# Output tiles of a gated delta-rule layer: beside all chunks of the recurrence, or beside the last two and behind it

## The chip, the cores and the metric

The kernel runs on one core of a Trainium2 chip. The core has five engines that work at the same time, each through its own list of instructions and strictly in the order of that list: TensorE (PE in the profile, matmuls and transposes; PEld is its loading of weights), VectorE (DVE), ScalarE (ACT), GpSimd (POOL) and SyncE (SP), which here only issues DMA transfers. Engines wait for each other by semaphores. The metric is the device time of one execution in microseconds (us); the time of a kernel is the median of its runs.

## The reference

The program is one inference step of a two-layer hybrid encoder for 2048 prompt tokens and 32 sample tokens of width 1024. The change lies in the first layer, a gated delta rule with 8 heads of width 128. Cut to what matters:

```python
def delta_layer(x, conv_buf, s0, w_in, conv_w, a_log, dt_bias, norm_w, w_out, ln_g, ln_b):
    proj = x @ w_in
    qkv, new_buf = causal_conv(proj[..., :CONV_DIM], conv_buf, conv_w)
    z = proj[..., CONV_DIM:CONV_DIM + A_VW].reshape(b, l, A_HEADS, A_DV)
    ...
    o, s_new = gated_delta_rule(q, k, v, g, beta, s0.astype(jnp.float32))
    o = o * lax.rsqrt(jnp.mean(o * o, -1, keepdims=True) + RMS_EPS) * norm_w * jax.nn.silu(z)
    out = o.reshape(b, l, A_VW).astype(x.dtype) @ w_out
    return layer_norm(DN_ALPHA * x + out, ln_g, ln_b), new_buf, s_new.astype(x.dtype)

# gated_delta_rule, one block of positions after another, for each head
    lower = jnp.where(strict, jnp.einsum('nbhik,nbhjk->nbhij', kbeta, kc) * decay, 0.0)
    # u, w: solutions of (lower + 1) against v * beta and k * beta * exp(gcum)
    def step(s, xs):
        v_new = ui - jnp.einsum('bhck,bhkv->bhcv', wi, s)
        o = jnp.einsum('bhck,bhkv->bhcv', qd, s) + jnp.einsum('bhij,bhjv->bhiv', ai, v_new)
        s = s * gl[..., None, None] + jnp.einsum('bhck,bhcv->bhkv', kd, v_new)
        return s, o
```

The second layer (windowed attention with a gate) takes the first layer's output `h` and begins with projections of it.

## The kernel before

The program goes through stages. `P1` makes the projections of the first layer. `z`, the gate product, is a projection of its own (`P1.z`, L211 to L225): for each of 8 heads and each block of 416 tokens 24 matmuls of 128x416, then tanh on ACT and two operations on DVE. Blocks 0, 1 and 2 of `z` are done before the delta stage, blocks 3 and 4 are put beside it.

The delta stage (`Delta.run`) goes through 17 chunks: 16 of 128 prompt tokens and one of 32 sample tokens. What a chunk needs is made two chunks ahead, in these steps:

- `lower` (L400 to L405): the products `g` of the keys on PE, in two halves; DVE multiplies them by the decays `E` into `npr`; after the second half ACT copies the diagonal 32x32 blocks to `nb`.
- `chain` (L414 to L423): DVE transposes `nb` to `L`; then 62 small steps on POOL, two for each of 31 rows (`tm`, L421, and `Tt`, L423), invert all those blocks.
- `spread` (L479 to L492): when the chain has ended, DVE transposes `Tt` to `tcp` and `ucp`, and ACT copies them into the matrices `t` and `u` in four pieces each.
- `invert` (lines L509 to L534, tile `bps`): small matmuls on PE, with copies between them, put the 32x32 inverses together to 128x128.
- `turn_k`, `turn_v` and `inside` (L433 to L467): transposes of `k` and `v`, and the products `gq` of `q` and `k`.
- `errors` and `advance` (L544 to L581): the step itself, on the state `Sp`: `ks`, `vp`, `vs`, then `op` and `sp`, with `o` copied by ACT and its squares summed there.
- `scale` and `emit`: the normalized `o` is transposed, multiplied by `z` and stored as `s_g` (L611).

Buffers come from pools. `L`, `tm`, `nb` and others lie in a pool with one buffer, `Tt` in one with two. One buffer means that the next write to the tile waits until the last reader of the one before is done.

The output tiles (class `O1`) compute `layer_norm(ALPHA * x + out)` for 128 tokens each: 17 tiles. `fetch` (L726 to L730) loads `s_g` of a tile into `g` and the rows of `x` into `r`. `split` (L737, L738) splits `g` into `g_hi` (a cast on ACT) and `g_lo` (a subtraction, on POOL). `tile` has two halves of 512 columns; each is 8 k-steps of three matmuls 128x512 (L751 to L753: `g_hi` by `wo_hi`, `g_hi` by `wo_lo`, `g_lo` by `wo_hi`), and then DVE does the residual, the statistics and the normalization. Finally `turned` (L790 to L803) transposes the tile in eight pieces (L797, tile `tr`), ACT and DVE copy four of them each to `hT`, and `hT` is stored, since the next stage reads the tokens in its columns. `hT` and `g` share one buffer (tag `g` of the one-buffer pool). The transposes have a PSUM bank of their own, the products `po` two. The constructor loads the output weights in eight pieces (L699 to L701).

The next stage is `P2`, the second layer's projections; it loads `hT` by blocks of 416 tokens as `act_raw` (L860) and weights by `slab`. Two of its gate products (`gate(0, (0,))` and `gate(0, (1,))`) need only the first blocks of `hT` and are run among the last output tiles.

The order of the work is set in two ways. On DVE, ACT, POOL and SP a scheduler orders the instructions by a simulation of the program. On PE, in `with tc.manual_schedule(engines={PE})`, the order is that in which the code issues: the delta rule's steps, and between them a `Filler`. `Filler.give(us)` adds `us` to what is owed and draws the generator `beside()` until its steps, each of which names its own length, have paid for it. `beside()` is first the gate products of blocks 3 and 4, then the output tiles; an output tile waits until the chunk of the tile after it has been issued (`sent`). In `run` each step is followed by a call of `fill` with a share of `more`, 0.8 up to the last two chunks and 1.6 there. Behind the last chunk `filler.rest()` draws what is left.

Of the kernel before, what the change touches and what calls it, by code (L numbers as in the profile page):

```python
# [10 lines left out]
F32 = mybir.dt.float32  # L11
# [3 lines left out]
ALU = mybir.AluOpType  # L15
AX = mybir.AxisListType
PSUM = bass.MemoryType.PSUM
# [312 lines left out]
class Delta:  # L330
# [282 lines left out]

    def run(self, chunks, fill, done):

        n = len(chunks)
        at = lambda i: chunks[i] if i < n else None

# [31 lines left out]
        for i, ch in enumerate(chunks):  # L650
            nx, n2 = at(i + 1), at(i + 2)
            more = 0.8 if n2 else 1.6
            if n2:
# [24 lines left out]
            g = self.inside(n2, V) if n2 else iter(())  # L678
# [34 lines left out]
class OutNorm:  # L713
# [18 lines left out]
    def split(self, got, n):  # L732
        nc = self.nc
        g, r = got
        ghi = self.two.tile([128, KC, 128], F32R, tag="g_hi", name="g_hi")
        glo = self.two.tile([128, KC, 128], F32R, tag="g_lo", name="g_lo")
        nc.scalar.copy(ghi[:, :, :n], g[:, :, :n])  # L737
        nc.gpsimd.tensor_tensor(out=glo[:, :, :n], in0=g[:, :, :n], in1=ghi[:, :, :n], op=ALU.subtract)  # L738
        return ghi, glo, r
# [40 lines left out]
class O1:  # L780
    def __init__(self, tc, es, I, O, T, G):
        self.nc, self.I, self.T, self.G = tc.nc, I, T, G
        self.on = OutNorm(tc, es, "o1", "left", I, "a", 2)
        self.pt = new_pool(tc, es, "o1_pt", 1, PSUM, side="left")

# [3 lines left out]
    def turned(self, h, c0, row, n):  # L789
# [3 lines left out]
        for q in range(2):  # L793
            tr = self.pt.tile([128, 4, 128], F32, tag="tr", name="tr")
            for j in range(4):
                k = q * 4 + j
                nc.tensor.transpose(tr[:, j, :n], h[:n, k * 128:k * 128 + 128], self.G["ident"][:n, :n])  # L797
            if q == 0:
                nc.scalar.copy(hT[:, 0:4, :n], tr[:, :, :n])
            else:  # L800
                nc.vector.tensor_copy(hT[:, 4:8, :n], tr[:, :, :n])
                nc.sync.dma_start(T["hT"][:, :, c0:c0 + n].rearrange("h p t -> p h t"), hT[:, :, :n])
            yield 0.44  # L803

    def tiles(self, tiles, ready, more):
# [3 lines left out]
        got = self.on.split(self.fetch(*tiles[0]), tiles[0][2])  # L809
        for i, t in enumerate(tiles):  # L810
            while not all(ready(u) for u in tiles[i + 1:i + 2]):
                yield 1.0
# [11 lines left out]
            if i + 2 == len(tiles):  # L824
                yield from more(0)
        yield from more(1)
        yield from late


class P2:  # L830
# [3 lines left out]
    def __init__(self, tc, right, I, O, T):  # L834
# [8 lines left out]
        self.x = {}  # L843
        self.w = {}
        for b in (0, 1):
            self.load(b, self.resr)
# [336 lines left out]
def program(tc, I, O, T, G):  # L1183
# [10 lines left out]

    def beside():
        yield from p1.z((3, 4), zp, ("zth", "z"), p1.left_ps, nc.vector)
        left.close()
        o1.append(O1(tc, left, I, O, T, G))
        tiles = [(t * 128, t * 128, min(128, NT - t * 128)) for t in range(NTT)]
        yield 20.0  # L1200
        yield from o1[0].tiles(tiles, lambda t: t[0] in sent, first_gate)

    def first_gate(b):
        yield from p2.gate(0, (b,), p2.ps)

    filler = Filler(beside())
    chunks = [Chunk(t * 128, 128) for t in range(16)] + [Chunk(NP, NS)]

    def done(ch):
        sent.add(ch.t0)  # L1210

    with tc.manual_schedule(engines={mybir.EngineType.PE}):
        delta.run(chunks, filler.give, done)
        right.close()
        p2 = P2(tc, right, I, O, T)
        p2.slab(0, nc.gpsimd)
        p2.slab(1, nc.gpsimd)
        filler.rest()
    left.close()
    p2.open_left(left)  # L1220
    drain(p2.gate(1, (0, 1), p2.ps))
# [174 lines left out]
```

## Time and profile before

| what | value |
|---|---|
| time, runs | 2402.85, 2398.37, 2401.82 us; median 2401.82 |
| profiled execution | 2404.43 us, of which the span of its instructions 2402.4 |
| PE | 2228.8 us busy, 93% of the span |
| PEld | 2029.5 us, 84% |
| DVE | 1392.3 us, 58% |
| POOL | 929.5 us, 39% |
| ACT | 898.5 us, 37% |

The busy shares are means over stages with different limits. The page's table of 40 slices shows PE at nine tenths or more in most slices and at seven to eight in the slices from about 840 us on, where the delta stage runs; POOL is busy for five to seven tenths there. The stage lies between about 712 us (the first chunk's preparation) and 1521.6 us (the last matmul of an output tile).

Rows of the trace read as start, length, engine, line, operation, out<-in with the tiles' names, shape; in square brackets stands the idle time before the instruction and what ended it. Groups read as count, busy time, mean length in ns, and idle time before them with what ended it.

### The profile page before, as it was taken

To read this page: it belongs to the slowest core of one execution; us is meant where nothing else is said; L and a number is where in the kernel's file an instruction comes from. 1 tells how busy PE (TensorE), PEld (TensorE's weight loads), DVE (VectorE), ACT (ScalarE), POOL (GpSimd) and SP (SyncE) were. 2 spreads that over 40 slices of the span, in tenths; PEclk is the share of its full clock that TensorE was granted. 3 is DMA by queue.
4 is the path that set the end of the run, shared out by engine and by line. 5 is a ranking of instruction groups with operands and counts; after the bars stand their busy time and mean duration, and the time that the engine had idled before them with its cause. 6 is when DMAs were issued, how large, how long until landed. Compare 5 with 4: busy or idle time off the path is not lost. (4 is left out here: it accounts for less than half of the span.)

```text
span 2402.4 us, 36689 instructions
## 1 busy us (share of the span) xinstructions
PE 2228.8 (93%) x13778; PEld 2029.5 (84%) x13778; DVE 1392.3 (58%) x2648; ACT 898.5 (37%) x2197; POOL 929.5 (39%) x1413
## 2 busy tenths in 40 slices
PE   7999999999989968888878897999999998999997
PEld 5999999999988857777777785899999986788885
DVE  3676666544437667777766766413444225667874
ACT  3344444333224454545444432221111235444451
POOL 1422212111203356565766644103433134555663
PEclk9999999999999979999898998999999999999998
DMA  5111211121236374555454446422222266233221
GB/s 181 62 73 67 76 71 63 71 80 67 100 105 139 94 189 83 134 119 118 120 129 102 123 125 191 146 80 101 68 74 75 75 154 178 80 97 106 88 67 57
DMA packets 268593, 247.79 MB, mean 103 GB/s; under 512 B 67600, under 2 KB 243792, under 8 KB 265072
## 3 DMA queue, kind: packets, MB, share of 16 engines
q1 hardware_dynamic: 259168, 233.50, 34.1%
q10 hardware_dynamic: 9248, 11.96, 1.6%
q8 instruction: 108, 1.77, 0.3%
q14 instruction: 69, 0.57, 0.1%
HBM read 154.57 MB, written 91.20 MB: 102 GB/s over the span
## 5 line engine op out<-in xcount | busy, mean ns | idle before, releaser
L69 PE MATMUL ps<-act_hi,w_hi 128*128 128x416 f32 x2000 | 708.6, 355 | 2.7 <-ACT w_hi L50 2.0
L71 PE MATMUL ps<-act_hi,w_lo 128*128 128x416 f32 x2000 | 702.6, 352 | 0.0
L70 PE MATMUL ps<-act_lo,w_hi 128*128 128x416 f32 x2000 | 701.9, 351 | 0.2 <-DVE act_lo L61 0.2
L69 PEld LDWEIGHTS ps<-act_hi,w_hi 128*128 128x128 f32 x2000 | 376.2, 188 | 8.6 <-ACT w_hi L50 2.3
L70 PEld LDWEIGHTS ps<-act_lo,w_hi 128*128 128x128 f32 x2000 | 377.0, 189 | 4.6 <-DVE act_lo L61 0.6
L71 PEld LDWEIGHTS ps<-act_hi,w_lo 128*128 128x128 f32 x2000 | 376.1, 188 | 5.5
L51 POOL TENSOR_TENSOR w_lo<-w_raw,w_hi 128x1024 fp32r<-128x1024 f32 x54 | 143.7, 2661 | 609.5 <-ACT w_hi L50 557.9
L421 POOL TENSOR_TENSOR tm<-L,Tt 128x60 f32<-128x60 f32 (+26 forms) x496 | 184.9, 373 | 261.4 <-DVE L L414 194.6
L180 DVE SCALAR_TENSOR_TENSOR y<-R,convw,y 128x2083 f32<-128x2083 f32 x72 | 171.6, 2384 | 121.1 <-ACT y L178 119.8
L423 POOL TENSOR_TENSOR Tt<-Tt,tm 128x60 f32<-128x60 f32 (+26 forms) x496 | 195.0, 393 | 38.5
L1140 POOL TENSOR_TENSOR P<-P,sm 128x384 f32<-128x384 f32 (+2 forms) x128 | 103.5, 830 | 159.3 <-DVE sm L1017 85.1
L210 ACT COPY R<-ps 128x416 f32<-128x416 f32 (+1 forms) x144 | 61.4, 449 | 208.4 <-PE ps L71 184.2
L1013 ACT ACTIVATE P<-S,nm 128x192 f32<-128x192 f32 (+2 forms) x260 | 104.7, 420 | 90.9 <-DVE nm L1006 43.7
L50 ACT CAST w_hi<-w_raw 128x1024 fp32r<-128x1024 f32 x62 | 65.0, 1049 | 193.5 <-PE ps L70 154.8
L880 POOL TENSOR_TENSOR rs<-rs,sin 128x416 f32<-128x416 f32 x50 | 71.3, 1426 | 147.4 <-DVE rs L879 103.0
L751 PE MATMUL po<-wo_hi,g_hi 128*128 128x512 f32 (+1 forms) x272 | 120.1, 441 | 0.0
L753 PE MATMUL po<-wo_hi,g_lo 128*128 128x512 f32 (+1 forms) x272 | 109.5, 402 | 0.0
L752 PE MATMUL po<-wo_lo,g_hi 128*128 128x512 f32 (+1 forms) x272 | 109.3, 402 | 0.0
L1153 PE MATMUL ot<-pt,vd 128*128 128x256 f32 x372 | 98.8, 392 | 3.5 <-DVE graw L1156 1.6
L1038 PE MATMUL po<-wo_hi,g_hi 128*128 128x512 f32 x240 | 100.0, 417 | 1.3 <-ACT wo_hi L700 1.3
L1039 PE MATMUL po<-wo_lo,g_hi 128*128 128x512 f32 x240 | 96.9, 404 | 2.1 <-DVE wo_lo L701 2.1
L566 PE MATMUL op<-Sp,q 128*128 128x128 f32 (+1 forms) x272 | 61.6, 313 | 37.4 <-ACT o L570 30.8
(263 smaller groups left out, 4187.1 us busy)
## 6 DMA issues: line engine op xcount, KB each, us to landing
w_raw<-in_w_in SPq DMA_DIRECT2D x40, 512.0 KB
w_raw<-in_b_w_in SPq DMA_DIRECT2D x20, 512.0 KB
s_z<-z SPq DMA_DIRECT2D x40, 208.0 KB
s_bz<-za SPq DMA_DIRECT2D x40, 208.0 KB
s_bq<-ra SPq DMA_DIRECT2D x40, 208.0 KB
s_q<-y SPq DMA_DIRECT2D x8, 1024.0 KB
s_k<-y SPq DMA_DIRECT2D x8, 1024.0 KB
s_v<-y SPq DMA_DIRECT2D x8, 1024.0 KB
```

The costliest lines, as they stand in the source:

```text
L51: sub.tensor_tensor(out=lo[:], in0=raw[:], in1=hi[:], op=ALU.subtract)
L69: nc.tensor.matmul(ps, hi[:, k, :], xh[:, k, :], start=(k == 0), stop=False)
L70: nc.tensor.matmul(ps, hi[:, k, :], xl[:, k, :], start=False, stop=False)
L71: nc.tensor.matmul(ps, lo[:, k, :], xh[:, k, :], start=False, stop=(k == KC - 1))
L180: nc.vector.scalar_tensor_tensor(out=y[:], in0=R[:, j:j + W], scalar=self.convw[:, i, j:j + 1], in1=y[:], op0=ALU.mult, op1=ALU.add)
L421: P.tensor_tensor(out=tm[:n, i0:, :w], in0=L[:n, i0:, j:j + 1].to_broadcast(sh), in1=Tt[:n, j:j + 1, :w].to_broadcast(sh), op=ALU.mult)
L423: P.tensor_tensor(out=Tt[:n, i0:, :w], in0=Tt[:n, i0:, :w], in1=tm[:n, i0:, :w], op=ALU.subtract)
L751: nc.tensor.matmul(ps[:n], ghi[:, k, :n], w[0][:, k, cs], start=(k == 0), stop=False)
L752: nc.tensor.matmul(ps[:n], ghi[:, k, :n], w[1][:, k, cs], start=False, stop=False)
L753: nc.tensor.matmul(ps[:n], glo[:, k, :n], w[0][:, k, cs], start=False, stop=(k == KC - 1))
L1013: nc.scalar.activation(P[u], src, AF.Exp, bias=nm[:, u:u + 1], scale=1.0, accum_out=sm[:, u:u + 1])
L1140: nc.gpsimd.tensor_tensor(out=P[:, u, :nj], in0=P[:, u, :nj], in1=f.unsqueeze(1).unsqueeze(3).to_broadcast([128, nj, 2, 64]), op=ALU.mult)
```

## The change

One generator beside the delta rule becomes two, and the order on PE in the delta stage is given to the scheduler.

- `first` is the gate products of blocks 3 and 4, and the construction of `O1`. `run` draws it with `fill` in chunks 0 to 3 (`more` 0.4) and calls `first.rest()` at chunk 4.
- In chunks 4 to 14 `more` is 0. In chunks 15 and 16 `fill` draws `second`, the output tiles, with `more` 1.6.
- `delta.run` is outside the manual order of PE; only `second.rest()`, behind it, is inside.
- `g_lo` is made by DVE in place of POOL.
- The transposes of `turned` have no PSUM pool of their own: they use the pool `po` of the products (two banks), and behind the delta stage the two banks of `P2`.
- `P2` is built before `second.rest()`; its loads of `hT` (`load_right`) and the slabs 0 and 1 are issued at output tile 8, and its two gate products behind tile 15 and behind tile 16.

```diff
     def run(self, chunks, first, second, done):
+        fill = first.give
...
         for i, ch in enumerate(chunks):
             nx, n2 = at(i + 1), at(i + 2)
-            more = 0.8 if n2 else 1.6
+            if i == 4:
+                first.rest()
+            more = 0.4 if i < 4 else 0.0 if n2 else 1.6
+            if not n2:
+                fill = second.give
...
         nc.scalar.copy(ghi[:, :, :n], g[:, :, :n])
-        nc.gpsimd.tensor_tensor(out=glo[:, :, :n], in0=g[:, :, :n], in1=ghi[:, :, :n], op=ALU.subtract)
+        nc.vector.tensor_tensor(out=glo[:, :, :n], in0=g[:, :, :n], in1=ghi[:, :, :n], op=ALU.subtract)
...
         self.on = OutNorm(tc, es, "o1", "left", I, "a", 2)
-        self.pt = new_pool(tc, es, "o1_pt", 1, PSUM, side="left")
+        self.bank = lambda: self.on.pp.tile([128, 512], F32, tag="po", name="tr")
...
-            tr = self.pt.tile([128, 4, 128], F32, tag="tr", name="tr")
+            tr = self.bank()[:].rearrange("p (j t) -> p j t", j=4)
...
         for i, t in enumerate(tiles):
+            if i == 8:
+                yield from more(0)
...
             if i + 2 == len(tiles):
-                yield from more(0)
-        yield from more(1)
+                yield from more(1)
+        yield from more(2)
...
+
+    def load_right(self):
         for b in (0, 1):
             self.load(b, self.resr)
...
-    def beside():
+    def gated():
         yield from p1.z((3, 4), zp, ("zth", "z"), p1.left_ps, nc.vector)
         left.close()
         o1.append(O1(tc, left, I, O, T, G))
+
+    def outputs():
         tiles = [(t * 128, t * 128, min(128, NT - t * 128)) for t in range(NTT)]
-        yield 20.0
-        yield from o1[0].tiles(tiles, lambda t: t[0] in sent, first_gate)
-
-    def first_gate(b):
-        yield from p2.gate(0, (b,), p2.ps)
-
-    filler = Filler(beside())
+        yield from o1[0].tiles(tiles, lambda t: t[0] in sent, more)
+
+    def more(i):
+        if i == 0:
+            p2[0].load_right()
+            for j in range(2):
+                p2[0].slab(j, nc.gpsimd)
+        else:
+            yield from p2[0].gate(0, (i - 1,), p2[0].ps)
+
+    p2 = []
+    first, second = Filler(gated()), Filler(outputs())
...
+    delta.run(chunks, first, second, done)
+    right.close()
+    p2.append(P2(tc, right, I, O, T))
+    o1[0].bank = p2[0].ps
     with tc.manual_schedule(engines={mybir.EngineType.PE}):
-        delta.run(chunks, filler.give, done)
-        right.close()
-        p2 = P2(tc, right, I, O, T)
-        p2.slab(0, nc.gpsimd)
-        p2.slab(1, nc.gpsimd)
-        filler.rest()
+        second.rest()
     left.close()
+    p2 = p2[0]
     p2.open_left(left)
```

In the new kernel the lines of the output tiles lie six lines lower (`po` is L757 to L759, `tr` L803, the load of `g` L733, the store of `hT` L808, that of `h` L829) and the load of `act_raw` is L870. The scheduler places the first output tiles by its own simulation: of the 272 k-steps it sets 62 on PE beside chunks 1 to 4, none beside chunks 5 to 13, and 210 from chunk 14 on.

The second half of a chunk between 5 and 13 on PE; `bps` are the steps of `invert`, `vtr` and `gq` the preparation two chunks ahead, `po` the output tile. Before:

```order
L447 MATMUL vtr<-ident,v 128x128 x4
L522 MATMUL bps<-y_9716,u_5052 64x64 x8
L462 MATMUL gq<-q,k 128x128 x4
L751 MATMUL po<-wo_hi,g_hi 128x512
L752 MATMUL po<-wo_lo,g_hi 128x512
L753 MATMUL po<-wo_hi,g_lo 128x512
```

The same place now:

```order
L447 MATMUL vtr<-ident,v 128x128 x4
L522 MATMUL bps<-y_9619,u_5052 64x64 x8
L462 MATMUL gq<-q,k 128x128 x8
L528 MATMUL bps<-ta,npr 64x64 x8
L533 MATMUL bps<-u,ta 64x64 x8
L609 MATMUL otr<-ident,o 128x128 x8
```

The output matmuls are gone from between the delta rule's own, and the halves of `gq` and of `otr` stand together.

On ACT, from the end of one chain to the copy that the next one waits for, before (`t` and `u` are the pieces of `spread`, `hT` belongs to an output tile):

```order
L553 COPY vs<-vp 128x512 x2
L491 COPY t_5050<-tcp 32x8x32 x4
L570 COPY o<-op 128x512
L417 COPY Tt<-tinit 128x256
L492 COPY u_5052<-ucp 32x8x32 x4
L799 COPY hT<-tr 128x512
L581 ACTIVATE vn,Xo<-o 128x128 x4
L405 COPY nb<-npr 32x256 x4
```

The same place now:

```order
L553 COPY vs<-vp 128x512
L491 COPY t_5050<-tcp 32x8x32 x4
L417 COPY Tt<-tinit 128x256
L492 COPY u_5052<-ucp 32x8x32 x4
L553 COPY vs<-vp 128x512
L405 COPY nb<-npr 32x256 x4
```

In this chunk `hT`, `o` and the squares left the way to `nb`, and one `vs` came into it; in two chunks of three a copy of `o` and its squares still stand there.

On PE in chunk 1 of the new kernel, the first output tile (L757, L758) and the chunk's own step (`op`):

```order
L551 MATMUL vp<-rho,u 128x128 x4
L757 MATMUL po<-wo_hi,g_hi 128x512
L758 MATMUL po<-wo_lo,g_hi 128x512
L757 MATMUL po<-wo_hi,g_hi 128x512
L758 MATMUL po<-wo_lo,g_hi 128x512
L566 MATMUL op<-Sp,q 128x128
L567 MATMUL op<-vs,at 128x128
```

Four output matmuls, which need the output weights, stand ahead of `op`; before, no output matmul was in this chunk.

On SP among the last output tiles, before:

```order
L729 DMA r<-in_x 128x1024
L802 DMA s_hT<-hT 128x8x128
L821 DMA s_h<-r 128x1024
L727 DMA g<-s_g 128x8x128
L860 DMA act_raw<-s_hT 128x2x416
```

Now:

```order
L808 DMA s_hT<-hT 128x8x128
L735 DMA r<-in_x 128x1024
L733 DMA g<-s_g 128x8x128
L829 DMA s_h<-r 128x1024
```

The store of a tile's `hT` still stands ahead of the load of the next `g`, and the loads of `act_raw` have left this stretch, where tile follows tile.

More of the change, by code (lines that the diff above doesn't have):

```diff
@@ L612, in emit, with run @@
             yield "otr"
-    def run(self, chunks, fill, done):
+    def run(self, chunks, first, second, done):
         n = len(chunks)
+        fill = first.give
         at = lambda i: chunks[i] if i < n else None
```

## The prediction

> **What bounds the kernel now.** I read the page for the span, then a table of busy time by stage (stretch in us, its length, busy us and count for PE, PEld, DVE, ACT and POOL, then granted clock, DMA share, GB/s):
>
> ```profile
> span 2402.4 us, 36689 instructions
> ```
> ```profile
> 712.00:831.60 119.60, 102.75 (x764) 97.64 (x764) 81.48 (x180) 52.11 (x139) 37.14 (x95) 0.93 0.48 114
> 831.60:994.70 163.10, 124.20 (x1093) 111.65 (x1091) 113.18 (x230) 84.10 (x236) 105.45 (x254) 0.87 0.56 131
> 994.70:1366.00 371.30, 314.05 (x2682) 279.76 (x2680) 266.70 (x619) 175.48 (x522) 233.85 (x565) 0.93 0.51 121
> 1366.00:1401.90 35.90, 32.06 (x301) 27.70 (x300) 24.41 (x69) 14.31 (x46) 23.96 (x66) 0.95 0.35 97
> 1401.90:1460.00 58.10, 58.10 (x338) 45.94 (x336) 38.52 (x126) 14.46 (x47) 14.79 (x30) 1.00 0.58 168
> 1460.00:1521.60 61.60, 46.95 (x207) 34.66 (x207) 36.47 (x68) 13.63 (x18) 25.91 (x13) 0.86 0.56 175
> ```
>
> The rows are: A, the first two chunks' preparation and chunk 0, beside the gate products; B, chunks 1 to 4; C, chunks 5 to 13; D, chunk 14, then chunks 15 and 16, then what is left of the output tiles. The change touches only these 809.6 us. In A and chunk 15/16 PE is close to full; in C it is idle for 57 of 371 us, so something else sets the pace there. The two ends of C are chunk 5's first `ks` matmul and chunk 14's:
>
> ```profile
> 994.75 0.38 PE L544 MATMUL ks<-Sp,k 128*128 128x128 f32 x1
> ```
> ```profile
> 1366.04 0.38 PE L544 MATMUL ks<-Sp,k 128*128 128x128 f32 x1
> ```
>
> So nine chunks take 371.3 us, 41.25 each. The waits of C name the pacemaker (engine, line, releaser: us, times, longest):
>
> ```profile
> POOL tm L421 <- DVE L L414: 51.3, 5, 13.5
> DVE tcp L479 <- POOL Tt L423: 47.2, 8, 7.3
> ```
>
> POOL waits for `L`, and DVE waits for `Tt`: a loop. POOL's 62 small steps per chunk (`chain`) need `L`, which has one buffer; `L` is made by DVE from `nb`, and on DVE's queue `tcp`, which waits for the end of the chain before, stands ahead of the `npr` that `nb` copies. Chunk by chunk, then: chain, restart, chain. One turn, from its timeline (start, us, engine, operation, idle before):
>
> ```profile
> 1179.78 0.26 POOL L421 TENSOR_TENSOR tm<-L,Tt 128x31 f32<-128x31 f32 x1 [9.96 <-DVE L L414]
> ```
> ```profile
> 1211.67 0.68 DVE L479 STREAM_TRANSPOSE tcp<-Tt 128x256 f32<-128x256 f32 x1 [6.62 <-POOL Tt L423]
> ...
> 1220.48 0.69 DVE L401 TENSOR_TENSOR npr<-g,E 128x512 f32<-128x512 f32 x1 [0.58 <-PE g L400]
> 1222.88 2.08 DVE L414 STREAM_TRANSPOSE L<-nb 128x1024 f32<-128x1024 f32 x1 [1.71 <-ACT nb L405]
> ```
> ```profile
> 1212.39 1.64 ACT L491 COPY t<-tcp 32x256 f32<-32x256 f32 x4 [7.22 <-DVE tcp L479]
> 1214.04 0.40 ACT L417 COPY Tt<-tinit 128x256 f32<-128x256 f32 x1
> 1214.36 1.64 ACT L492 COPY u<-ucp 32x256 f32<-32x256 f32 x4
> ...
> 1221.20 1.64 ACT L405 COPY nb<-npr 32x256 f32<-32x256 f32 x4 [2.80 <-DVE npr L401]
> ```
> ```profile
> 1225.10 0.26 POOL L421 TENSOR_TENSOR tm<-L,Tt 128x31 f32<-128x31 f32 x1 [13.46 <-DVE L L414]
> ```
>
> The chain runs 1179.78 to 1211.67, 31.9 us (one 2.4 us `g_lo` of the output tile inside it), and the restart takes 13.4 us more, of which several are spent because the second `g` came late on PE. An output tile's 11 us of matmuls hide in the rest. The change takes them out of a stage that PE does not bound, and puts most of them where PE does.
>
> **C, nine chunks without output work: -36 us.** The restart left to itself is `tcp` 0.68, four `t` copies 1.64, the start value of `Tt` 0.40, four `u` copies 1.64, `nb` 1.64, `L` 2.08: 8.1 us and a few handovers, 8.7. In the new order a copy of `o` and four squares stand ahead of `nb` on ACT in two chunks of three (groups of C: busy us, mean ns of one):
>
> ```profile
> L581 ACT ACTIVATE vn<-o 128x128 f32<-128x128 f32 x72 | 21.4, 298 | 0.5
> L581 ACT ACTIVATION_READ_ACCUMULATOR vn<-o 128x1 f32 x72 | 13.5, 187 | 0.0
> L570 ACT COPY o<-op 128x512 f32<-128x512 f32 x18 | 10.5, 584 | 8.6 <-PE op L567 8.3
> ```
>
> Together 0.58 + 4 x 0.49 = 2.5 us; some of it fits beside DVE's steps, and I take 1.5 on the mean: 10.2. The chain: with little output work on DVE and none on POOL inside it, a full chunk's was
>
> ```profile
> 1350.63 0.26 POOL L421 TENSOR_TENSOR tm<-L,Tt 128x31 f32<-128x31 f32 x1 [8.11 <-DVE L L414]
> ...
> 1376.98 0.20 POOL L423 TENSOR_TENSOR Tt<-Tt,tm 128x8 f32<-128x8 f32 x1
> ...
> 1386.55 0.25 POOL L421 TENSOR_TENSOR tm<-L,Tt 32x31 f32<-32x31 f32 x1 [1.16 <-DVE L L414]
> ```
>
> 26.6 us, and the period to the next 35.9. I take 27.0 + 10.2 = 37.2 a chunk: 4.05 x 9 = 36 us saved. Bounds: above, 41.25 (no gain), if another wait takes the place; below, a chain that also sheds one such stall as this:
>
> ```profile
> 1189.87 2.76 POOL L423 TENSOR_TENSOR Tt<-Tt,tm 128x76 f32<-128x76 f32 x1
> ```
> ```profile
> 1190.40 0.67 DVE L466 TENSOR_TENSOR k<-k,gb 128x512 f32<-128x512 f32 x1
> 1191.00 0.68 DVE L467 TENSOR_TENSOR q<-q,gb 128x512 f32<-128x512 f32 x1
> ```
>
> A POOL step that takes 0.2 to 0.3 us in the rows above took 2.76 while DVE ran `k` and `q`, which read two SBUF tiles each. One stall of some 2.4 us less makes the chain 24.2 and the period 24.2 + 8.7 = 32.9, a gain of 75. I stay at 27.0, since the delta rule's own such DVE operations remain in every chunk. [...]
>
> **D, from chunk 14 on: +88 us.** The output tiles' matmuls by stretch (the rows of line L751 alone: PE us and count, one per k-step of three matmuls), and the last tile's first and last matmul:
>
> ```profile
> 994.70:1366.00 371.30, 57.71 (x128) 25.21 (x128) 0.93 0.51 121
> 1366.00:1401.90 35.90, 6.09 (x14) 2.64 (x14) 0.95 0.35 97
> 1401.90:1521.60 119.70, 41.80 (x98) 18.09 (x98) 0.93 0.57 172
> ```
> ```profile
> 1510.25 0.39 PE L751 MATMUL po<-wo_hi,g_hi 128*32 128x512 f32 x1
> ```
> ```profile
> 1521.56 0.39 PE L753 MATMUL po<-wo_hi,g_lo 128*32 128x512 f32 x1
> ```
>
> A tile's 48 matmuls take 11.3 us on PE, 0.72 us a k-step. Now 14 + 98 = 112 k-steps stand after chunk 14's start; in the new order 210 do (62, almost four tiles, were drawn forward beside chunks 1 to 4, none stand in C). 98 x 0.72 = 71 us. The new order has 13 more groups of four `hT` transposes there; at 0.6 us a group,
>
> ```profile
> 1449.33 0.60 PE L797 MATMUL tr<-ident,r 128*128 128x128 f32 x4
> ```
>
> 8 us. PE's idle time in D is 3.8 + 0 + 14.7 = 18.5 us by the stage rows. In the new kernel: 10 us early in chunk 14, where no tile may yet start, and in the tail some 1.5 us for each of 12 tiles, 28 in all, 9.5 more. The 1.5 us come from the one buffer that `g` and `hT` share:
>
> ```profile
> 1478.66 0.36 SPq L802 DMA_DIRECT2D s_hT<-hT  x1
> ...
> 1482.94 0.36 SPq L727 DMA_DIRECT2D g<-s_g  x1
> ```
> ```profile
> 1487.13 1.04 ACT L737 CAST g_hi<-g 128x1024 fp32r<-128x1024 f32 x1 [11.71 <-DMA g<-s_g]
> ```
>
> Store of `hT` 4.3 us, load of `g` 4.2, `g_hi` 1.0, `g_lo` on DVE (by POOL's 2.4 us at most, by `g_hi`'s 1.0 at least; I take 1.3), copies of `hT` and issue about 2.5: 13.3 us a turn against 11.9 of PE. The banks for the transposes, now two, cost nothing there. ACT's in-order waits for `act_raw`, the next stage's input, lie in the same tail and are in the 28. Bounds of D: +70 (no idle in the tail) to +140 (the tail's pace of now, see the third rival).
>
> **B, chunks 1 to 4: +8 us.** Four tiles beside them as beside chunks 3 to 6 before, but tile 0 now stands on PE ahead of chunk 1's `op`, and the output weights come only so fast:
>
> ```profile
> 840.05 0.82 SPq L699 DMA_DIRECT2D wo_raw<-in_a_w_out  x2
> ```
> ```profile
> 876.16 1.04 ACT L700 CAST wo_hi<-wo_raw 128x1024 fp32r<-128x1024 f32 x1 [0.19 <-DMA wo_raw<-in_a_w_out]
> ```
>
> 37 us for eight pieces through two buffers. PE queues chunk 1's `op`, `sp` and second `g` behind them; SP has chunk 3's `k` behind five of them, where it went first. That delays one chain by some 10 us, of which I give back a little because `g_lo` leaves POOL. Bounds -4 and +25 (the 37 us less what chunk 1 waits already, 47 for a usual 39).
>
> **A: -5 us.** PE's order is now the scheduler's, and more gate products stand ahead of the first `g`, where PE idles; A has 17 us of PE idle, so -12 to +5. `first.rest()` at chunk 4 finds nothing left of the gate products. The earlier loads and slabs for the next stage (`load_right`, `slab`) lie beside PE's full tail: nothing, or the `act_raw` wait counted above.
>
> **Sum.** -5 + 8 - 36 + 88 = +55 us on the profiled execution's 2404.4, 2459; that execution was 2.6 us above the median of the three runs, so 2457.
>
> **Rivals.** *Faster:* the output tile's DVE work was what slowed the chain: two stalls like the 2.76 us row's leave it, 26.6 - 4.8 = 21.8, and with the bare restart of 8.7 the period is 30.5 us. C is then -97, and the sum -5 + 8 - 97 + 88 = -6 us: 2396. It decides from a period of 31.1 us on (C -91). Against it: the 26.6 us row, and that most of the two-input operations are the delta rule's own. *PE's clock:* with its filler gone PE is idle for some 15 of 37 us in C, and the granted clock, 0.87 in B where it idles most, falls further; the 22 us of the delta rule's PE work in a chunk grow towards 41 and the period stays: C 0, sum +91, 2493. Against it: no PE work stands in the restart itself. [...] *A slow tail:* the stretch to 1521.6 held about three and a half tiles in 61.6 us, 17 to 18 each; at that pace twelve tiles cost 50 us more than I take: 2507. For it: the shared buffer and ACT's waits remain; against it: the transposes had one bank and have two, and `g_lo` leaves POOL. *No change:* gain and loss cancel within 0.2% (about 5 us, what a measurement of this kernel can tell).
>
> **Chances.** Forecast 0.60, faster 0.13, clock 0.10, slow tail 0.13, no change 0.04. The range runs from 2418 (C at its bound of -75 and the rest as taken: +16) to 2512, which takes in the clock rival and the slow tail's figure; below it lie the faster rival and no change, 17 in 100. Faster 0.13, same 0.04, slower 0.83.
>
> **What would show it.** In the new profile: the first `tm` of successive chunks 37 us apart in chunks 5 to 13, with no output matmul there; PE busy for 55 to 65% of that stretch; chunk 14's start 25 to 40 us earlier than 1366; the last output matmul 45 to 65 us later than 1521.6; twelve tiles some 13.5 us apart at the end. I am wrong if the period is under 33 us, or if the tail is paced by something other than PE.

## The result and the profile after

The changed kernel takes 2435.49 us (median of 4 runs, 2433.7 to 2442.17) against 2400.62 us before: a ratio of 1.015, 95% interval 1.0128 to 1.0173. It is slower, by 35 us; the forecast was 2457, in a range of 2418 to 2512. The profiled span is 2434.6 us, 32.2 more than before, and all of it lies ahead of the last output matmul, which ends that much later; behind it both kernels take 881 us.

The same table by stage as for the kernel before (stretch, length, busy us and count of PE, PEld, DVE, ACT, POOL, granted clock, DMA share, GB/s), and the rows that set its borders:

```profile
712.00:838.10 126.10, 103.99 (x787) 97.68 (x787) 84.32 (x187) 59.44 (x156) 46.89 (x124) 0.89 0.51 130
838.10:1002.50 164.40, 144.16 (x1165) 127.04 (x1163) 125.90 (x272) 79.98 (x227) 85.15 (x229) 0.92 0.54 135
1002.50:1329.20 326.70, 236.81 (x2234) 214.54 (x2232) 205.68 (x441) 162.56 (x506) 195.21 (x553) 0.85 0.37 86
1329.20:1371.10 41.90, 38.17 (x323) 32.31 (x323) 25.70 (x69) 14.07 (x43) 28.12 (x86) 0.96 0.33 91
1371.10:1433.00 61.90, 61.29 (x336) 50.05 (x336) 44.59 (x129) 13.47 (x38) 0.52 (x3) 0.96 0.59 176
1433.00:1553.80 120.80, 114.99 (x530) 88.09 (x529) 83.52 (x210) 23.68 (x37) 22.33 (x10) 0.96 0.60 184
```
```profile
1002.50 0.27 PE L544 MATMUL ks<-Sp,k 128*128 128x128 f32 x1
```
```profile
1329.16 0.58 PE L544 MATMUL ks<-Sp,k 128*128 128x128 f32 x1
```
```profile
1553.86 0.39 PE L759 MATMUL po<-wo_hi,g_lo 128*32 128x512 f32 x1
```

| stretch | before | after | difference | forecast |
|---|---|---|---|---|
| A, to chunk 1 | 119.6 | 126.1 | +6.5 | -5 |
| B, chunks 1 to 4 | 163.1 | 164.4 | +1.3 | +8 |
| C, chunks 5 to 13 | 371.3 | 326.7 | -44.6 | -36 |
| D, from chunk 14 to the last output matmul | 155.6 | 224.6 | +69.0 | +88 |
| sum | 809.6 | 841.8 | +32.2 | +55 |

In C a chunk takes 36.3 us in place of 41.25. The mean chain there went from 30.2 to 26.8 us and the mean restart, from the end of a chain to the start of the next, from 11.2 to 9.9, over nine turns each. One turn of the loop (start, us, engine, operation, idle before):

```profile
1156.39 0.67 DVE L479 STREAM_TRANSPOSE tcp<-Tt 128x256 f32<-128x256 f32 x1 [6.09 <-POOL Tt L423]
1156.95 0.65 DVE L401 TENSOR_TENSOR npr<-g,E 128x512 f32<-128x512 f32 x1
1157.88 0.66 DVE L401 TENSOR_TENSOR npr<-g,E 128x512 f32<-128x512 f32 x1
1164.68 1.97 DVE L414 STREAM_TRANSPOSE L<-nb 128x1024 f32<-128x1024 f32 x1 [2.65 <-ACT nb L405]
```
```profile
1157.09 1.65 ACT L491 COPY t<-tcp 32x256 f32<-32x256 f32 x4 [5.79 <-DVE tcp L479]
...
1159.56 1.64 ACT L492 COPY u<-ucp 32x256 f32<-32x256 f32 x4
1161.22 0.59 ACT L570 COPY o<-op 128x512 f32<-128x512 f32 x1
...
1163.02 1.63 ACT L405 COPY nb<-npr 32x256 f32<-32x256 f32 x4
```
```profile
1129.44 0.26 POOL L421 TENSOR_TENSOR tm<-L,Tt 128x31 f32<-128x31 f32 x1 [10.45 <-DVE L L414]
...
1156.15 0.20 POOL L423 TENSOR_TENSOR Tt<-Tt,tm 128x8 f32<-128x8 f32 x1
1166.79 0.26 POOL L421 TENSOR_TENSOR tm<-L,Tt 128x31 f32<-128x31 f32 x1 [10.43 <-DVE L L414]
```

The chain takes 26.9 us and the restart 10.4; both `npr` are done at 1158.5, four and a half us before ACT comes to `nb`. In this turn ACT's queue (`t`, `u`, `o` and its squares) sets the restart. The longest wait of POOL and the longest of DVE in C are the same two as before (engine, line, releaser: us, times, longest):

```profile
POOL tm L421 <- DVE L L414: 89.0, 9, 10.5
...
DVE tcp L479 <- POOL Tt L423: 46.0, 9, 6.6
```

In D PE is busy for 38.2 + 61.3 + 115.0 = 214.5 of 224.6 us: 10 us idle, where the kernel before idled 18.5 of 155.6. Its waits behind chunk 14:

```profile
PE po L757 <- ACT g_hi L743: 2.5, 2, 1.8
PE ps L803 <- issue: 2.0, 2, 1.6
PE po L759 <- DVE g_lo L744: 1.9, 4, 0.5
```

### The profile page after: what moved, and what is told of

Read it like the earlier page. It is cut to its first block, busy times and chain, and to the rows that moved or that the text cites. A ratio compares the mean times of both kernels' runs of the same rounds, so it can differ in the third digit from the quotient of the medians.

```text
span 2434.6 us, 36721 instructions
## 1 busy us (share of the span) xinstructions
PE 2247.7 (92%) x13778; PEld 2041.5 (84%) x13778; DVE 1408.0 (58%) x2665; ACT 898.0 (37%) x2197; POOL 865.4 (36%) x1396
## 4 chain that ended last, share of the span: by engine, by line
PE 66%; POOL 12%; DMA 8%; DVE 6%; ACT 4%; issue 4%; SPq 0%; DVEq 0%; ACTq 0%; POOLq 0%
PE ps L69 14%; PE ps L71 14%; PE ps L70 14%; POOL Tt L423 6%; POOL tm L421 5%; PE ot L1163 3%; PE po L1048 2%; PE po L1049 2%; PE po L1050 2%; PE S L1142 2%; PE po L757 2%; PE po L759 2%; PE po L758 1%; PE tr L1157 1%; DMA g<-s_g 1%
## 5 line engine op out<-in xcount | busy, mean ns | idle before, releaser
L421 POOL TENSOR_TENSOR tm<-L,Tt 128x60 f32<-128x60 f32 (+26 forms) x496 | 173.2, 349 | 308.1 <-DVE L L414 258.1
L423 POOL TENSOR_TENSOR Tt<-Tt,tm 128x60 f32<-128x60 f32 (+26 forms) x496 | 182.7, 368 | 38.9
L757 PE MATMUL po<-wo_hi,g_hi 128*128 128x512 f32 (+1 forms) x272 | 113.3, 417 | 3.8 <-ACT g_hi L743 3.8
L759 PE MATMUL po<-wo_hi,g_lo 128*128 128x512 f32 (+1 forms) x272 | 110.1, 406 | 1.9 <-DVE g_lo L744 1.9
L758 PE MATMUL po<-wo_lo,g_hi 128*128 128x512 f32 (+1 forms) x272 | 109.6, 403 | 0.0
L1050 PE MATMUL po<-wo_hi,g_lo 128*128 128x512 f32 x240 | 95.6, 398 | 0.0
```

Of the source, the lines that this page charges most:

```text
L421: P.tensor_tensor(out=tm[:n, i0:, :w], in0=L[:n, i0:, j:j + 1].to_broadcast(sh), in1=Tt[:n, j:j + 1, :w].to_broadcast(sh), op=ALU.mult)
L423: P.tensor_tensor(out=Tt[:n, i0:, :w], in0=Tt[:n, i0:, :w], in1=tm[:n, i0:, :w], op=ALU.subtract)
L757: nc.tensor.matmul(ps[:n], ghi[:, k, :n], w[0][:, k, cs], start=(k == 0), stop=False)
L759: nc.tensor.matmul(ps[:n], glo[:, k, :n], w[0][:, k, cs], start=False, stop=(k == KC - 1))
L1050: nc.tensor.matmul(ps[:n], glo[:, k, :n], w[0][:, k, cs], start=False, stop=(k == KC - 1))
```

## The experiments

Starts of chunk 5, of chunk 14 (the first `ks` matmul of each) and of the last output matmul, in us of each profile; the period is the difference of the first two over nine. A profile is that of one execution, the time the median of all; the profiled executions of the longer chain and of the tiles drawn from chunk 4 on took 2485.3 and 2388.2 us, 6 and 10 above their medians.

| kernel | time | chunk 5 | chunk 14 | period | last output matmul |
|---|---|---|---|---|---|
| before | 2400.6 | 994.7 | 1366.0 | 41.3 | 1521.6 |
| changed | 2435.5 | 1002.5 | 1329.2 | 36.3 | 1553.9 |
| changed, longer chain | 2478.9 | 1009.8 | 1368.8 | 39.9 | 1599.5 |
| changed, `g_lo` on POOL | 2452.4 | 1001.9 | 1328.3 | 36.3 | 1567.7 |
| changed, one late bank | 2452.3 | 1005.0 | 1331.3 | 36.3 | 1571.7 |
| changed, PE's order by hand | 2472.4 | 986.4 | 1310.1 | 36.0 | 1586.9 |
| changed, tiles drawn from chunk 4 | 2378.3 | 1009.3 | 1372.9 | 40.4 | 1501.9 |
| changed, transposes' own bank | 2369.6 | 1004.0 | 1373.4 | 41.0 | 1490.9 |
| the same, `g_lo` on POOL | 2378.9 | 1004.7 | 1373.3 | 41.0 | 1497.3 |
| the same, `lower` first | 2389.1 | 1004.7 | 1375.1 | 41.2 | 1502.7 |
| before, `g_lo` on DVE | 2418.2 | 998.2 | 1378.3 | 42.2 | 1536.0 |
| before, no normalization | 2387.3 | 998.3 | 1358.7 | 40.1 | 1511.1 |
| before, a quarter of the matmuls | 2382.0 | 989.9 | 1354.4 | 40.5 | 1504.1 |
| before, `lower` first | 2390.0 | 987.8 | 1350.8 | 40.3 | 1504.7 |

### Does the loop of chain and restart set the pace of C?

The changed kernel with every fourth product of the chain issued twice:

```diff
         for j in range(31):
...
-            P.tensor_tensor(out=tm[:n, i0:, :w], in0=L[:n, i0:, j:j + 1].to_broadcast(sh),
-                            in1=Tt[:n, j:j + 1, :w].to_broadcast(sh), op=ALU.mult)
+            for _ in range(2 if j % 4 == 0 else 1):
+                P.tensor_tensor(out=tm[:n, i0:, :w], in0=L[:n, i0:, j:j + 1].to_broadcast(sh),
+                                in1=Tt[:n, j:j + 1, :w].to_broadcast(sh), op=ALU.mult)
```

> The changed kernel with every fourth product of the chain on POOL issued twice (8 more instructions a chain, some 0.35 us each, the result unchanged). Theory (the loop of chain and restart paces): the chain of each of 9 chunks in C is 2.8 us longer and so is the period: C +25, with the other chunks +35 to +42: 2473. Rival (the loop has slack, PE at its lower clock or ACT paces): within 5 us of 2435.

2478.91 us, ratio to before 1.033 (1.0313 to 1.0346), 43.4 above the changed kernel. The period rose by 3.6 us. POOL's groups in C, of the changed kernel and of this one (groups with count, busy us, mean ns, idle before; the second stretch is 1000 to 1360):

```profile
L423 POOL TENSOR_TENSOR Tt<-Tt,tm 128x60 f32<-128x60 f32 (+24 forms) x276 | 100.9, 366 | 21.6
L421 POOL TENSOR_TENSOR tm<-L,Tt 128x60 f32<-128x60 f32 (+24 forms) x277 | 94.6, 341 | 109.9 <-DVE L L414 89.0
```
```profile
L422 POOL TENSOR_TENSOR tm<-L,Tt 128x60 f32<-128x60 f32 (+12 forms) x347 | 118.1, 340 | 108.2 <-DVE L L414 81.7
L424 POOL TENSOR_TENSOR Tt<-Tt,tm 128x60 f32<-128x60 f32 (+24 forms) x276 | 112.6, 408 | 21.6
```

POOL's work grew by (118.1 + 112.6 - 100.9 - 94.6) / 9 = 3.9 us a chunk and the period by 3.6. By the turns the chain grew from 26.8 to 31.3 us on the mean, and the restart shrank from 9.9 to 9.1. There is hardly any slack beside the chain: the loop paces C of the changed kernel, as the prediction had it.

### What holds the output tiles behind the delta stage?

Two kernels bring the tiles back beside the chunks. The first draws them in the code from chunk 4 on (the loads and slabs of `P2` go behind the delta stage, since its buffers are made there):

```diff
-            more = 0.4 if i < 4 else 0.0 if n2 else 1.6
-            if not n2:
+            more = 0.4 if i < 4 else 0.8 if n2 else 1.6
+            if i >= 4:
                 fill = second.give
```

> The changed kernel with the output tiles drawn from chunk 4 on (0.8 a step) in place of the last two chunks alone; the early loads and slabs of the next stage go behind the delta stage, since their buffers do not exist before. PE's order stays the scheduler's. Theory: the period of chunks 5 to 13 returns to 40 to 41 (+35 to +42 us), 146 k-steps and 18 groups of transposes leave the stretch behind chunk 14 (-105 -11): about 2360, below the kernel before. Rival (the gain in C came from PE's order, not from the absent tiles): the period stays below 38 and the time is 2330 or less. Rival (with tiles in the scheduler's order the chunks get much longer): over 2400.

2378.25 us, ratio 0.9913 (0.989 to 0.9936): 57 us faster than the changed kernel and 23 faster than before. The period is 40.4, as forecast; the time is 18 above the 2360 that was expected.

The second leaves the drawing as changed and only gives the transposes their own bank again:

```diff
-        self.bank = lambda: self.on.pp.tile([128, 512], F32, tag="po", name="tr")
+        self.pt = new_pool(tc, es, "o1_pt", 1, PSUM, side="left")
...
-            tr = self.bank()[:].rearrange("p (j t) -> p j t", j=4)
+            tr = self.pt.tile([128, 4, 128], F32, tag="tr", name="tr")
...
-    o1[0].bank = p2[0].ps
```

> The changed kernel with the transposes' own PSUM pool of one bank, as before the change, and nothing else undone. In PE's order this alone brings a tile's 16 k-steps back beside every chunk from 1 to 15, although the code still draws no tile in chunks 4 to 14. Theory: it behaves as the kernel that draws the tiles from chunk 4 on: 2378, 2365 to 2400. Rival (what counts is where the code draws the tiles): 2435.

2369.57 us, ratio 0.9862 (0.9842 to 0.9882). The output matmuls by stretch, rows of its line L757 alone (PE us and count, one per k-step), chunks 1 to 4, C, and D:

```profile
840.40:1004.00 163.60, 25.94 (x64) 12.06 (x64) 0.93 0.54 135
1004.00:1373.40 369.40, 59.13 (x144) 27.42 (x144) 0.93 0.50 126
1373.40:1491.00 117.60, 26.74 (x64) 11.46 (x64) 0.88 0.51 148
```

A tile stands beside each of the nine chunks, though the code draws none there: the scheduler moves them forward by itself. In the changed kernel the transposes of the 13 tiles drawn there take banks of `P2`, and `P2` is built after the delta stage's pools are closed; those tiles stay behind, and with a bank of their own they do not. So `more = 0.0` alone does not hold the tiles back: it takes the bank as well. In the first of the two kernels the transposes have no bank of their own either, and drawing the tiles earlier was enough. The second is the fastest that was run, 66 us below the changed one: the period goes from 36.3 to 41.0 (C +42.7), D from 224.6 to 117.5 (-107).

### What is the tail's density worth?

One bank for the transposes, opened behind the delta stage, so that the tiles stay behind it:

```diff
-    o1[0].bank = p2[0].ps
+    t1s = ExitStack()
+    t1 = new_pool(tc, t1s, "o1_t1", 1, PSUM, side="right")
+    o1[0].bank = lambda: t1.tile([128, 512], F32, tag="tr", name="tr")
```

> The changed kernel with one PSUM bank for the transposes of the output tiles behind the delta stage, in place of two; the tiles stay where they are (none in chunks 5 to 13). Theory (as predicted: the second bank costs and brings nothing in the tail): 2433 to 2442. Rival (the second bank is what makes the tail dense; PE waited 14.2 us for hT in the 119.7 us behind chunk 14 before, some five tiles): about 3 us more for each of 12 tiles, 2470.

2452.26 us, ratio 1.0207 (1.0181 to 1.0234), 17 above the changed kernel. Between theory and rival: D is 240.4 us, 15.8 longer, with 22.9 us of PE idle in place of 10.1. PE's first wait there (engine, line, releaser: us, times, longest):

```profile
PE tr L803 <- ACT hT L805: 16.4, 8, 4.2
```

The second four transposes of a tile wait until ACT has copied the first four out of the one bank; this wait is absent from the changed kernel's list.

`g_lo` back on POOL:

```diff
-        nc.vector.tensor_tensor(out=glo[:, :, :n], in0=g[:, :, :n], in1=ghi[:, :, :n], op=ALU.subtract)
+        nc.gpsimd.tensor_tensor(out=glo[:, :, :n], in0=g[:, :, :n], in1=ghi[:, :, :n], op=ALU.subtract)
```

> The changed kernel with g_lo back on POOL. Theory: no output tile stands in chunks 5 to 13, so the period there stays 36.3; in the first four tiles some 2.4 us each go into a chain, and in the tail g_lo lies on the way from g to the matmuls, 1.1 us more a tile where that way is late at all: 2437 to 2452, I say 2442. Rival (g_lo's engine made the tail as dense as it is): the tail's tiles fall back to 17 us, +50: 2485.

2452.44 us, ratio 1.0217 (1.0202 to 1.0232), also 17 above, just over the upper end of what was expected. C is unchanged, as it must be, and D is 239.3 us, 14.7 longer:

```profile
PE po L759 <- POOL g_lo L744: 8.3, 5, 3.0
PE po L757 <- ACT g_hi L743: 6.2, 2, 4.1
```

Each of these two parts of the change keeps some 15 us out of the tail. For the second bank the prediction took nothing; for `g_lo` 1.1 us a tile, which is 13 for twelve. The way from a store of `hT` to the next is a loop of its own (the store, the load of `g` into the same buffer, `g_hi`, `g_lo`, the copies of `hT`), and it has to fit into a tile's PE time. Behind the delta stage the stores of the changed kernel follow each other in 15.8, 15.4, 14.5, 12.8, 12.4 and 11.6 us, with 5.8 us of PE idle in about the same stretch. One of these turns on SP's queue:

```profile
1503.40 0.37 SPq L808 DMA_DIRECT2D s_hT<-hT  x1
1508.12 0.37 SPq L733 DMA_DIRECT2D g<-s_g  x1
...
1515.79 0.37 SPq L808 DMA_DIRECT2D s_hT<-hT  x1
```

In this turn and the next it just fits: PE idles 0.3 us in the two.

### What did the scheduler's order on PE do?

The changed kernel with PE's order by hand in the delta stage too:

```diff
-    delta.run(chunks, first, second, done)
-    right.close()
-    p2.append(P2(tc, right, I, O, T))
-    o1[0].bank = p2[0].ps
     with tc.manual_schedule(engines={mybir.EngineType.PE}):
+        delta.run(chunks, first, second, done)
+        right.close()
+        p2.append(P2(tc, right, I, O, T))
+        o1[0].bank = p2[0].ps
         second.rest()
```

> The changed kernel with PE's order written by hand in the delta stage too, as before the change, so that no output tile comes beside chunks 1 to 4. Theory: 62 k-steps and 16 transposes more stand behind chunk 14 (62 x 0.72 + 2 = 47 us), chunks 1 to 4 lose the waits for the output weights (-10 to -15), the period of C stays near 36: 2470, 2460 to 2485. Rival (the scheduler's order on PE is what shortened the period): period 38 to 40, 2490 to 2510.

2472.4 us, ratio 1.0289 (1.0268 to 1.0311), as expected. All 272 k-steps stand in D, which is 276.8 us (+52.2); chunk 5 begins at 986.4, 16.1 us earlier than in the changed kernel and 8.3 earlier than before. So the scheduler's order, with the four tiles that it put beside chunks 1 to 4, costs 16 us up to there and saves 52 in D. Of the 16, 10.7 are lost by the start of chunk 1 (838.1 against 827.4), before the first output matmul. The period without tiles is 36.0 by hand and 36.3 by the scheduler: the short period does not come from the scheduler's order.

### What in a tile's work lengthens the period?

Between the traces of before and of the changed kernel the period differs by 5 us, of which 3.4 lie in the chain and 1.3 in the restart. POOL's busy time in C fell by 4.3 us a chunk; half of that is `g_lo`, the other half shorter steps of the chain (381 to 341 ns on the mean for `tm`, 393 to 366 for `Tt`). Three kernels take one part each of the tile's work from the kernel before, a fourth moves `lower`. First, `g_lo` on DVE (the diff above, turned round):

> The kernel before with g_lo made by DVE, nothing else. Theory (chain and restart pace chunks 5 to 13): the 2.4 us that POOL spends on g_lo leave the inside of a chain in every second chunk or so; DVE's g_lo, with two SBUF inputs, stalls the chain for at most its own 1.3 us. The period falls from 41.25 to between 39 and 41, the time by 2 to 20 us: 2390. Rival (another wait ends last, g_lo was beside it): 2396 to 2405, period unchanged.

2418.19 us, ratio 1.008 (1.006 to 1.01): neither theory nor rival, it is 17 us slower. POOL's busy time in C fell from 233.9 to 215.1 us, 2.1 a chunk, but the restart, from the start of `tcp` to the end of `L`, grew from 11.0 to 13.4 us on the mean of the turns; the chain fell from 30.2 to 28.7 alone. In the worst turn the second `g` came 14 us behind `tcp`:

```profile
1129.04 0.66 DVE L479 STREAM_TRANSPOSE tcp<-Tt 128x256 f32<-128x256 f32 x1 [5.63 <-POOL Tt L423]
...
1140.17 0.69 DVE L401 TENSOR_TENSOR npr<-g,E 128x512 f32<-128x512 f32 x1 [9.57 <-PE g L400]
...
1143.79 0.67 DVE L401 TENSOR_TENSOR npr<-g,E 128x512 f32<-128x512 f32 x1
...
1147.10 2.05 DVE L414 STREAM_TRANSPOSE L<-nb 128x1024 f32<-128x1024 f32 x1
```

What the chain gains, the restart loses, and more: in this turn `op`, the transposes and six output matmuls still stood ahead of the two `g` on PE when the chain had ended. That this is the reason in the other turns was not shown. In its profile C is 8.8 us longer than before, chunk 5 begins 3.5 later and D is 2.2 longer.

Second, without the last four DVE operations of a tile (the normalization of the first layer is left out):

```diff
             for c in range(2):
                 cs = slice(c * 512, c * 512 + 512)
-                V.scalar_tensor_tensor(out=r[:n, cs], in0=r[:n, cs], scalar=mv[:n, 0:1], in1=tabs[0][:n, cs],
-                                       op0=ALU.subtract, op1=ALU.mult)
-                V.scalar_tensor_tensor(out=r[:n, cs], in0=r[:n, cs], scalar=rs[:n, 0:1], in1=tabs[1][:n, cs],
-                                       op0=ALU.mult, op1=ALU.add)
```

> The kernel before without the last four operations of an output tile on DVE (the normalization by mean, scale and shift of the first layer is left out); all else stays. They read two SBUF tiles each, 0.7 us. Theory (such operations stall the chain for their whole length): 4 x 0.7 = 2.8 us a chunk leave the chain, C is 18 to 27 us shorter, the time 2375 to 2383. Rival (they lie beside waits of POOL, or the restart takes over): within 6 us of 2401.

2387.27 us, ratio 0.9939 (0.9918 to 0.9959), 13 to 15 below before. C is 360.5 us, 10.8 shorter, where 18 to 27 were expected. The operations do hold up the chain or the restart, by 1.2 us a chunk of the 2.6 that they take (23.6 us in C of the kernel before); POOL's busy time fell by 1.4 us a chunk.

Third, with 36 of the 48 matmuls of each first-layer tile left out:

```diff
             for k in range(KC):
-                nc.tensor.matmul(ps[:n], ghi[:, k, :n], w[0][:, k, cs], start=(k == 0), stop=False)
-                nc.tensor.matmul(ps[:n], ghi[:, k, :n], w[1][:, k, cs], start=False, stop=False)
-                nc.tensor.matmul(ps[:n], glo[:, k, :n], w[0][:, k, cs], start=False, stop=(k == KC - 1))
+                if k in (0, KC - 1):
+                    nc.tensor.matmul(ps[:n], ghi[:, k, :n], w[0][:, k, cs], start=(k == 0), stop=False)
                    nc.tensor.matmul(ps[:n], ghi[:, k, :n], w[1][:, k, cs], start=False, stop=False)
                    nc.tensor.matmul(ps[:n], glo[:, k, :n], w[0][:, k, cs], start=False, stop=(k == KC - 1))
```

> The kernel before with 36 of the 48 matmuls of each output tile of the first layer left out (k-steps 0 and 7 alone remain); DVE's, ACT's and POOL's work for the tile stays. Theory (the tile's place in PE's queue holds the second g of the next chunk, and with it nb and L): the restart falls to 9 or 10 us, the period of C to 37 or 38 although g_lo and the normalization still lie beside the chain; with some 60 us less PE work behind chunk 14 the time is 2300 to 2320. Rival (the tile's work on DVE and POOL sets the period): period 40 to 41, time 2335 to 2350.

2382.04 us, ratio 0.9912 (0.9886 to 0.9937). The rival holds for C: the period falls by only 0.8 us, to 40.5, so it is not the tile's matmul time that sets it. The gain of 60 us that was expected behind chunk 14 failed too: the two stretches, C and D, are (columns as in the table by stage)

```profile
989.90:1354.40 364.50, 268.98 (x2395) 243.08 (x2392) 268.54 (x621) 176.20 (x524) 224.27 (x558) 0.85 0.53 123
1354.40:1504.10 149.70, 98.90 (x590) 77.42 (x588) 102.73 (x264) 42.47 (x111) 66.24 (x114) 0.71 0.55 160
```

so D is 149.7 us against 155.6, with PE idle for a third of it. So the tail before the change had another limit close behind PE. The one bank and `g_lo` on POOL, which cost the changed kernel 15 us each, were both in it; which of them it was, this kernel does not show. The rival's time, 2335 to 2350, failed by this too.

Fourth, `lower` in front of `advance`:

```diff
-            for s in (a, low, a, low, a, a):
+            for s in (low, low, a, a, a, a):
```

> The kernel before with both halves of lower (the products g of the chunk two ahead) drawn in front of the four steps of advance, in place of between them; all else stays. On PE both g now stand ahead of op. Theory (a late second g lengthens the restart): restart 9.5 in place of 11, the time 2380 to 2392. Rival (op, sp and what waits for them come later and another wait takes its place): 2398 to 2410.

2390.02 us, ratio 0.9962 (0.9946 to 0.9978). As expected by the time; the restart is 10.1 us on the mean in place of 11.0, and the period 40.3. The early chunks gain as much: chunk 5 begins 6.9 us earlier.

The normalization and the matmuls, each taken out alone, take 1.2 and 0.8 us from the 5 us that a tile costs its chunk; `g_lo` moved to DVE adds 1.0, and `lower` in front takes 0.9. No kernel took out several at once, so what makes up the 5 us is only in part shown.

### Two tries to go below 2370

Both start from the changed kernel with the transposes' own bank. With `lower` in front of `advance`:

> The changed kernel with the transposes' own bank (2370 in its own run) and both halves of lower in front of advance. Theory: its restart of 13 us falls to 10 to 11, a gain of 15 to 25 us: 2350. Rival (the restart there waits for other things than the second g): 2365 to 2375.

2389.1 us, ratio 0.9948 (0.9927 to 0.9968): slower than without by 19.5 (the profiled executions by 12.4). The restart did not fall: it is 13.4 us on the mean against 12.6. The period is 41.2 against 41.0, and D grew by 10 us. Which wait took the place of the second `g` is open.

With `g_lo` on POOL:

> The changed kernel with the transposes' own bank, and g_lo back on POOL. Theory (g_lo on DVE lengthens the restart by more than it takes from the chain, as in the kernel before, where it cost 17 us; it pays in a dense tail, and this kernel has little tail): the restart falls from 12.6 by 1 to 2 us, the chain grows by 2, the tail by some 3: between 2355 and 2368. Rival (here too g_lo on DVE pays, as it did by 17 us in the changed kernel): 2380 to 2387.

2378.89 us, ratio 0.99 (0.9883 to 0.9916): slower by 9. The period is the same 41.0: from the end of a chain to the start of the next it takes 12.3 us on the mean in place of 12.7, and the chain 28.4 in place of 27.8. D is 124.1 in place of 117.5. Here `g_lo` on DVE pays, where in the kernel before it cost, and neither sign was what the theory had expected. What decides it was not shown.

One of its restarts is the shortest of all, 1.95 us. Here `npr` and `nb` were made while the chain before still ran, and on DVE `L` stands ahead of `tcp`:

```profile
1349.75 2.06 DVE L414 STREAM_TRANSPOSE L<-nb 128x1024 f32<-128x1024 f32 x1 [0.41 <-POOL tm L421]
...
1351.76 0.72 DVE L479 STREAM_TRANSPOSE tcp<-Tt 128x256 f32<-128x256 f32 x1
```
```profile
1351.95 0.27 POOL L421 TENSOR_TENSOR tm<-L,Tt 128x31 f32<-128x31 f32 x1 [1.95 <-DVE ln_y L321]
```

So most of a restart is not forced by the data: it comes from an order in which `tcp` and ACT's copies of it stand ahead of the next `nb` and `L`. No kernel with `L` ahead in every chunk was run.

## Why the prediction was right, and where not

**Sign and mechanism: right;** the forecast time lies 21.5 us above the measured one. By stage the gain in C came out 8.6 us larger than forecast, the loss in D 19 smaller, A 11.5 longer and B 6.7 shorter. Output tiles left a stage that PE does not bound and went where PE does. The loop as pacemaker, the gain in C and PE's work in D were read from the trace of before, and the run with the longer chain bears the loop out.

**C, -36 against -44.6.** The step is the period of 37.2 = 27.0 + 10.2, mis-sized by 0.9 us: the chains measure 26.6 to 26.9 us but for the first, the restarts 10.4 to 10.5 in two chunks of three and 8.8 in the third, 9.9 on the mean; the last one, ahead of the chain of the 32 sample tokens, takes 7.2. The turn of 26.6 us in the trace of before was the right row, and so was the order on ACT. The sign of PE's busy share failed: 55 to 65% was forecast for C, 72% measured, 26.3 us a chunk in place of 22, at a granted clock of 0.85.

**D, +88 against +69.** PE's work was right: 214.5 - 137.1 = 77.4 us more, forecast 71 + 8. The step that failed is the idle time: 28 us taken, 10.1 measured, of which 3.7 in chunk 14, where 10 were taken, and 6.4 behind it, where 18 were. The 18 were 1.5 us for each of twelve tiles. But five of them stand among the delta rule's own matmuls of chunks 14 to 16, with 0.6 us of PE idle in all. The six behind them idle 5.8 us together, 1.0 each: their turn for the buffer shared by `g` and `hT` is 13.7 us on the mean (13.3 forecast), and PE is busy for 12.7 of a tile (11.9 forecast). That the banks "cost nothing there" holds, but only with two: with one, D is 15.8 us longer, a gain that the sum did not have as a term. D's lower bound of +70 was missed by a us, since it kept 10 us idle in chunk 14.

**A and B, +3 against +7.8.** Neither term came out, and that they miss by only 5 us together is luck. In A PE's new order did bring chunk 0 forward, by 15.0 us (its first `ks` at 783.4 in place of 798.4; by hand it stands at 797.2). But the same order sets a `bps` (L509) ahead of chunk 1's `ks`, and this `bps` needs `t`, and so the end of a chain (waits from 826 to 866 us):

```profile
PE bps L509 <- ACT t L491: 9.2, 1, 9.2
```

That is 9.2 of the 21.5 us that chunk 0 takes longer. A's bounds of -12 to +5 missed its +6.5; the prediction did not ask what the new order sets ahead of `ks`. In B the mechanism, the load of the output weights moved up, held, on another engine: I priced it in chunk 1's queue on PE, where the first output matmul waited 1.3 us; ACT's queue holds casts of the weights and the first tile's `g_hi`, which wait for their loads, ahead of `vs`, and one restart took 35 us, in place of 10.5:

```profile
POOL tm L421 <- DVE L L414: 34.9, 1, 34.9
ACT wo_hi L706 <- DMA wo_raw<-in_a_w_out: 11.4, 6, 3.4
```

The chain ahead of it had begun 15 us earlier than before, so the next one starts 10.2 us later: the "some 10 us" of the prediction, by another sum. That chain then takes 26.5 us where it took 35.9, and B ends 1.3 us longer.

**The rivals.** *Faster* asked for a period of 31.1 us; it is 36.3, and the chain came down to the 26.6 us that the trace of before had shown once, no further. *PE's clock*: the granted clock in C did fall, from 0.93 to 0.85, with PE idle for 90 of 327 us. Behind a wait of PE its `ks` took longer: the first of chunk 14 took 0.58 us and the next seven 0.42 each, where chunk 5's, behind output matmuls, took 0.27 and 0.28, and just ahead of the slow ones stood

```profile
1327.27 1.97 PE L609 MATMUL otr<-ident,o 128*128 128x128 f32 x8 [3.16 <-DVE o L600]
```

The first `ks` of chunks 6 to 13 took 0.58 us each as well, with 5.1 to 5.6 us of idle time ahead of their `otr`. But the period fell all the same: in the turn shown the restart waits for nothing of PE's; both `npr`, which read PE's `g`, were done 4.5 us before ACT came to `nb`. *A slow tail*: 12 tiles at 17.5 us were forecast to cost 50 more; behind the last matmul of chunk 16 they follow each other in 12.0 to 16.6 us, the longest with a gate product of `P2` in between. The second bank and `g_lo` on DVE hold off 15.8 and 14.7 us of the 50, each taken back alone; both together were not.

**The tile's normalization on DVE.** Its four operations keep DVE busy for 23.6 us in C of the kernel before (16 of 769 and 16 of 777 ns on the mean). Taking those alone out of that kernel made C 10.8 us shorter. They count, but less than their whole length, and C's gain has other parts.

## What to carry to other kernels

Work that fills the gaps of a stage paced by a loop is not free, but it is cheap: here a tile cost its chunk 4.7 us (41.0 against 36.3) and some 12 us behind it. Moving such filler out shortens the loop visibly and loses more at the end; compare the two prices, not the stage with itself. And when a scheduler orders the work, ask of every buffer that an edit re-homes when that memory comes to exist: banks taken from a later stage pinned the 13 tiles that the code draws behind the present one, and giving them one of their own made the kernel 1.4% faster than before the change.

## What was not expected of the hardware

Eight more POOL instructions a chain, 2.6 us of busy time, cost 3.6 us of period, and the other steps grew too (`Tt` 366 to 408 ns on the mean of the groups shown); why they grew is open. And in the kernel with a quarter of the matmuls the granted clock was 0.71 in D, where the kernel before had 0.86 to 1.00, while the stretch barely became shorter (149.7 against 155.6 us): with less work, 98.9 us of PE busy against 137.1, the granted clock was lower too.
